# Strassen's scheme for half of the columns of a down projection, in a kernel for a two-layer trunk

## The chip, the cores and the metric

The kernel runs on one core of one Trainium2 chip. The metric is the device time in microseconds of one execution. The engines are TensorE (PE in the profile; PEld is its weight load), VectorE (DVE), ScalarE (ACT), GpSimd (POOL) and the sync engine's queue (SP), which issues the transfers of the weights. All data is float32. PE multiplies in the form fp32r, and each operand is split into a high part (hi, a copy in fp32r) and a low part (lo, the rest).

## The reference

Two layers over 256 tokens of width 2048. Each has a token mixer (a causal convolution in the first, a state-space layer with a gated output in the second) and then an MLP of width 8192:

```python
D_MODEL = 2048; SEQ = 256; DEPTH = 2; D_FF = 4 * D_MODEL

def mlp(h, w_up, w_down):
    a = jax.nn.relu(h @ w_up)
    return (a * a) @ w_down

def reference(x, ...):
    for i in range(DEPTH):
        h = rms_norm(x, mix_norm[i])
        x = x + (conv_module(h, ...) if i % 2 == 0 else ssm_module(h, ...))
        h = rms_norm(x, mlp_norm[i])
        x = x + mlp(h, mlp_w_up[i], mlp_w_down[i])
    return rms_norm(x, final_norm)
```

## The kernel before

`x` stays in SBUF as two blocks of 128 tokens by 2048 columns. Every dense projection is a list of steps (`self.steps`). One step is one piece of a weight of 1 MB: 8 row blocks of 128 by 256 columns for the up projection (`add_f`), 4 row blocks by 512 columns for the down projection (`add_t`). Each step has two halves of 128x1024 elements.

`run_steps` goes through the halves in order and keeps two kinds of work ahead of PE. `load` issues the transfers of the next four steps from the SP queue, into three raw buffers of a whole step. `split` makes hi on ACT (L118) and lo on DVE (L125; on POOL for the steps in `pool_lo`) for the next four halves; hi and lo have four buffers each. So the split of a half can begin when the matmuls of the half four places earlier have freed its buffer. The instructions of one engine run in the order in which a scheduler put them when the program was built; a tile framework adds the semaphores.

A down step multiplies in `mm_t` (L222 to L224): for each row block and each token block, three matmuls of 512 columns (activation hi by weight hi, hi by lo, lo by hi), 12 in a half. An up step (`mm_f`, L199 and L202) has 8 matmuls of 512 and 8 of 256 columns in a half.

The MLP takes the 8192 inner columns in eight row slices of 1024. `up(s)` makes slice s in four quarters of 256 columns; `relu2` (L807 to L812, and the hi and lo in L237 and L238) turns each quarter's result into squared activations `rT[s]`. `down(s)` multiplies them into four column slices of 512 columns, with one accumulator each in PSUM, which `add_x` adds to `x` on DVE (L820):

```python
        up(0)
        for s in range(1, nsl):
            up(s)
            down(s - 1)
        down(nsl - 1)
```

The second layer's MLP is the last large stage of the program.

Of the kernel before, what the change touches and what calls it, by code (L numbers as in the profile page):

```python
# [18 lines left out]
P = 128  # L19
EPS = 1e-6  # L20
D = 2048
T = 256
# [14 lines left out]
class Trunk:  # L37
    def __init__(self, ctx, tc, a, out):
# [10 lines left out]
        self.ms = pool("ms", 4, space=PSUM)  # L49
        self.dram = pool("dram", 1, space=DRAM)  # L50
        self.steps = []
        self.pending = []
        self.bg = []
        self.rate = self.credit = 0
        self.raws, self.parts = {}, {}
        self.loaded = 0
# [9 lines left out]
    def t4(self, shape, name="t4"):  # L66
        return self.tmp.tile(shape, F32, tag="t4", name=name)

# [11 lines left out]
    def add(self, view, shape, consume, pre=None):  # L80
        self.steps.append((view, shape, consume, pre))

    def add_f(self, w2d, k0, c0, consume, pre=None):
        self.add(w2d[k0 * P:(k0 + 8) * P, c0:c0 + 256].rearrange("(k p) n -> p k n", p=P), [P, 8, 256], consume, pre)
# [9 lines left out]
    def load(self, i, half=None):  # L94
        view, shape, _, _ = self.steps[i]
        for kind in self.before_load.pop(i, ()):
            self.table(*kind)
        if not half:
            self.raws[i] = self.w.tile(shape, F32, tag="raw", name="raw", bufs=3)
        raw = self.raws[i]  # L100
        nk = shape[1] // 2
        k = slice(0, shape[1]) if half is None else slice(half * nk, half * nk + nk)
        if len(shape) == 4:
            for j in range(shape[2]):
                self.fetch(raw[:, k, j, :], view[:, k, j, :])
        else:
            self.fetch(raw[:, k], view[:, k])
        self.loaded = i + 1

    def split(self, h, urgent=True):  # L110
        i, half = divmod(h, 2)
        raw = self.raws[i] if half == 0 else self.raws.pop(i)
        nk = raw.shape[1] // 2
        sl = raw[:, half * nk:(half + 1) * nk]
        hi = self.w.tile([P, nk] + list(raw.shape[2:]), F32R, tag="hi", name="hi", bufs=4)
        lo = self.w.tile([P, nk] + list(raw.shape[2:]), F32R, tag="lo", name="lo", bufs=4)
        with self.tc.high_priority(offset=URGENT if urgent else 0):
# [41 lines left out]
    def run_steps(self):  # L159
        n = 2 * len(self.steps)  # L160
        ns = 0
        for h in range(n):
# [7 lines left out]
            while self.loaded < min(len(self.steps), i + 4):  # L170
# [4 lines left out]
            if half == 0 and pre is not None:  # L175
                pre()
            hi, lo = self.parts.pop(h)
            consume(hi, lo, half)
            self.tick()
            self.pop_bg(self.rate)  # L180
# [504 lines left out]
    def mlp(self, layer, last_slice, last_block, hooks=None):  # L685
# [3 lines left out]

        def up(s):  # L690
            for q in range(4):
                for kc in range(2):
                    def consume(hi, lo, half, q=q, kc=kc):
                        if kc == 0 and half == 0:
                            if q == 0:
                                rT[s] = self.blk_tile([P, 8, 2, T], F32R, name="rT")
                            rT["acc"] = self.acc2()
                        A = rT["acc"]
                        self.mm_f([A[:, 0], A[:, 1]], self.hT, hi, lo, kc * 8 + half * 4,
                                  kc == 0 and half == 0, kc == 1 and half == 1)  # L700
                        if kc == 1 and half == 1:
                            if s == 0 and q == 1 and layer == 0:
                                self.rate = 2.75
                            if s == 0 and q == 0:
                                self.after(1, lambda: self.relu2(A, rT[s], 2 * q))
                            else:
                                self.relu2(A, rT[s], 2 * q)
                    self.add_f(w_up, kc * 8, s * 1024 + q * 256, consume)

        def down(s):  # L710
            for n in range(NS):
                by_block = s == nsl - 1 and n == NS - 1
                for kc in range(2):
                    def consume(hi, lo, half, n=n, kc=kc):
                        if kc == 0 and half == 0:
                            rT["acc"] = self.acc2()
                        k0 = kc * 4 + half * 2
                        self.mm_t(rT["acc"], lambda kk: rT[s][:, k0 + kk], hi, lo,
                                  kc == 0 and half == 0, kc == 1 and half == 1)
                        if kc == 1 and half == 1:  # L720
# [31 lines left out]
                    def consume_by_half(hi, lo, half, kc=kc):  # L752
# [3 lines left out]
                        for i, (b, c) in enumerate(((0, slice(0, 512)), (1, slice(0, 256)), (1, slice(256, 512)))):  # L756
                            with self.behind(self.mm_last):
                                self.mm_b(rT["acc"][i], lambda kk: rT[s][:, 2 * h + kk], hi, lo, b, c, h == 0, h == 3)
                            if h == 3:
# [6 lines left out]
                               (hooks or {}).get((nsl - 1 - s, n, kc)))  # L766

        up(0)
        for s in range(1, nsl):
            up(s)  # L770
            down(s - 1)
        down(nsl - 1)
# [43 lines left out]

    def tt(self, out, a, b, op):
# [788 lines left out]
```

## Time and profile before

| | |
|---|---|
| three runs | 1987.15, 1990.01, 1987.26 us; median 1987.26 |
| profiled execution, first to last instruction | span 1985.8 us (its time around the span isn't given apart) |
| mean granted clock of TensorE | 0.999 |
| PE, DVE, ACT, POOL busy | 99%, 71%, 48%, 14% of the span |
| second layer's MLP | about 1276 to 1976 us |
| transfers in the span | 428.49 MB, mean 216 GB/s |

An engine's busy time in the profile is the time in which one of its instructions ran. Matmuls overlap each other, so that their mean duration is longer than the distance from one start to the next. Rows of groups have the line, the engine, the operation and the tiles (out<-in), then the count, the busy time, the mean of one in ns, and the idle time just before them with what ended it. Rows of waits have who waited for whom, the time in all, how often, and the longest. Rows of the timeline have the start and the length in us. Rows of stretches have the busy time of PE, PEld, DVE, ACT and POOL, then the clock, the busy share of the transfer engines, and GB/s.

### The profile page before, as it was taken

What the parts mean: (1) busy time and instruction counts of PE and PEld (TensorE: products, weight loads), DVE (VectorE), ACT (ScalarE), POOL (GpSimd) and SP (SyncE); (2) the same over time, 40 slices, a digit from 0 to 9 for tenths busy, and PEclk for the clock granted to TensorE, in tenths of its full rate; (3) what the DMA queues carried; (4) which work ended last, traced back from release to release, by engine and by line L of the source; (5) the groups of instructions that cost most, each with busy time, mean ns of one, the idle gap of its engine ahead of it and who ended that gap; (6) DMA issues with size and microseconds to landing.
All of it is one profiled execution on the core that took longest, in us unless ns stands there. A gap on an engine that the chain in (4) does not pass through costs nothing.

```text
span 1985.8 us, 28885 instructions
## 1 busy us (share of the span) xinstructions
PE 1966.9 (99%) x11604; PEld 1687.0 (85%) x11604; DVE 1401.3 (71%) x1904; ACT 952.4 (48%) x1179; POOL 274.8 (14%) x252
## 2 busy tenths in 40 slices
PE   8999999999999999999999999999999999999998
PEld 8999788888888888888888788888888888888887
DVE  6899798888787777777558847565555565555655
ACT  6443655544444544444445445454444454444444
POOL 3998300000000221222010000000000000000000
PEclk9999999999999999999999999999999999999999
DMA  8767458667686877877898865665666656565653
GB/s 228 190 184 207 147 183 267 206 226 245 200 260 192 214 229 253 265 246 238 319 308 298 304 215 186 191 191 189 193 190 192 190 191 191 190 213 190 192 191 128
DMA packets 317030, 428.49 MB, mean 216 GB/s; under 512 B 9761, under 2 KB 211553, under 8 KB 313537
## 3 DMA queue, kind: packets, MB, share of 16 engines
q1 hardware_dynamic: 300976, 384.59, 61.6%
q0 software_dynamic: 12352, 37.49, 6.3%
q10 hardware_dynamic: 3568, 4.56, 0.8%
q8 instruction: 91, 1.49, 0.3%
q14 instruction: 43, 0.35, 0.1%
HBM read 400.08 MB, written 34.91 MB: 219 GB/s over the span
## 4 chain that ended last, share of the span: by engine, by line
PE 96%; DVE 2%; DMA 1%; issue 0%; SPq 0%; POOL 0%; ACT 0%; POOLq 0%; DVEq 0%; ACTq 0%
PE acc L199 24%; PE acc L222 15%; PE acc L223 15%; PE acc L224 15%; PE acc L202 12%; PE acc L213 3%; PE acc L212 3%; PE acc L211 3%; PE pk L484 1%; DMA Vt<-Vd 0%; SPq L92 0%; PE kp L1113 0%; PE xw L1254 0%; DMA raw<-in_conv_w_in_dram 0%; PE xt L254 0%
## 5 line engine op out<-in xcount | busy, mean ns | idle before, releaser
L118 ACT ACTIVATE hi<-raw 128x1024 fp32r<-128x1024 f32 x672 | 711.6, 1060 | 953.5 <-PE acc L224 510.2
L125 DVE TENSOR_TENSOR lo<-raw,hi 128x1024 fp32r<-128x1024 f32 x611 | 747.9, 1226 | 505.6 <-ACT hi L118 501.3
L199 PE MATMUL acc<-hT,hi 128*128 128x512 f32 x2048 | 514.4, 393 | 0.0
L199 PEld LDWEIGHTS acc<-hT,hi 128*128 128x128 f32 x2048 | 368.9, 189 | 68.0 <-issue 1.6
L222 PE MATMUL acc<-hi,rT 128*128 128x512 f32 x992 | 387.2, 391 | 0.0
L223 PE MATMUL acc<-lo,rT 128*128 128x512 f32 x992 | 386.4, 390 | 0.0
L224 PE MATMUL acc<-hi,rT 128*128 128x512 f32 x992 | 386.0, 389 | 0.0
L202 PEld LDWEIGHTS acc<-hT,lo 128*128 128x128 f32 x2048 | 279.6, 190 | 20.0
L202 PE MATMUL acc<-hT,lo 128*128 128x256 f32 x2048 | 286.3, 282 | 0.0
L222 PEld LDWEIGHTS acc<-hi,rT 128*128 128x128 f32 x992 | 186.3, 188 | 39.6 <-issue 1.6
L224 PEld LDWEIGHTS acc<-hi,rT 128*128 128x128 f32 x992 | 186.3, 188 | 39.1
L223 PEld LDWEIGHTS acc<-lo,rT 128*128 128x128 f32 x992 | 186.3, 188 | 38.0 <-issue 0.2
L125 POOL TENSOR_TENSOR lo<-raw,hi 128x1024 fp32r<-128x1024 f32 x60 | 143.1, 2402 | 31.3 <-ACT hi L118 24.8
L211 PE MATMUL acc<-hT,hi 128*128 128x256 f32 x512 | 146.1, 286 | 0.9 <-ACT hi L118 0.9
L212 PE MATMUL acc<-hT,hi 128*128 128x256 f32 x512 | 145.7, 286 | 0.3 <-DVE hT L259 0.3
L213 PE MATMUL acc<-hT,lo 128*128 128x256 f32 x512 | 145.5, 286 | 0.0
L829 DVE SCALAR_TENSOR_TENSOR cv<-vT,dw,cv 128x256 f32<-128x256 f32 x348 | 141.3, 486 | 2.2 <-ACT cv L527 1.7
L820 DVE TENSOR_TENSOR x<-x,acc 128x1024 f32<-128x1024 f32 (+1 forms) x72 | 83.6, 1161 | 27.6 <-PE acc L224 22.0
L211 PEld LDWEIGHTS acc<-hT,hi 128*128 128x128 f32 x512 | 98.9, 193 | 3.0 <-issue 1.6
L222 PE MATMUL acc<-hi,yT 128*128 128x512 f32 x256 | 101.1, 395 | 0.0
L212 PEld LDWEIGHTS acc<-hT,hi 128*128 128x128 f32 x512 | 98.8, 193 | 2.2 <-issue 1.6
L223 PE MATMUL acc<-lo,yT 128*128 128x512 f32 x256 | 99.9, 390 | 0.6 <-DVE lo L125 0.6
(285 smaller groups left out, 1722.9 us busy)
## 6 DMA issues: line engine op xcount, KB each, us to landing
raw<-in_mlp_w_up_dram SPq DMA_DIRECT2D x128, 1024.0 KB, 5.8
raw<-in_mlp_w_down_dram SPq DMA_DIRECT2D x128, 1024.0 KB, 5.2
raw<-in_ssm_w_glu_dram SPq DMA_DIRECT2D x32, 1024.0 KB, 5.5
raw<-in_conv_w_in_dram SPq DMA_DIRECT2D x60, 512.0 KB, 5.6
raw<-in_conv_w_out_dram SPq DMA_DIRECT2D x16, 1024.0 KB, 5.2
Vd<-bv POOLq DMA_DIRECT2D x16, 512.0 KB, 6.3
Md<-Kd POOLq DMA_DIRECT2D x32, 256.0 KB, 7.2
Wt<-Wd SPq DMA_DIRECT2D x8, 1024.0 KB, 10.1
```

The source lines that it names most:

```text
L118: self.nc.scalar.activation(hi, sl, AF.Copy)
L125: ins = eng.tensor_tensor(out=lo, in0=sl, in1=hi.bitcast(F32), op=ALU.subtract)
L199: mm(accs[m], lhsT=hi[:, kk, cs[m]], rhs=xT(k0 + kk), start=first and kk == 0, stop=False)
L202: mm(accs[m][:, 0:T], lhsT=lo[:, kk, cs[m]], rhs=xT(k0 + kk)[:, 0, :], start=False, stop=last and kk == 3)
L211: mm(accs[m], lhsT=hi[:, kk, c], rhs=x[:, 0, :], start=first and kk == 0, stop=False)
L212: mm(accs[m], lhsT=hi[:, kk, c], rhs=x[:, 1, :], start=False, stop=False)
L213: mm(accs[m], lhsT=lo[:, kk, c], rhs=x[:, 0, :], start=False, stop=last and kk == 3)
L222: mm(acc[:, b, :], lhsT=ak[:, 0, t], rhs=hi[:, kk, :], start=first and kk == 0, stop=False)
L223: mm(acc[:, b, :], lhsT=ak[:, 0, t], rhs=lo[:, kk, :], start=False, stop=False)
L224: self.mm_last = mm(acc[:, b, :], lhsT=ak[:, 1, t], rhs=hi[:, kk, :], start=False, stop=last and kk == 1)
L820: return self.nc.vector.tensor_tensor(out=out, in0=a, in1=b, op=op)
L829: return self.nc.vector.scalar_tensor_tensor(out=out, in0=a, scalar=s, in1=b, op0=op0, op1=op1)
```

## The change

In the second layer, for row slices 0 to 6, column slices 0 and 1 of the down projection are made together. The slice's activations A (256 tokens by 1024) are seen as 2 by 2 blocks: two token blocks by even and odd row blocks. The weight B (1024 by 1024 columns) is seen as 2 by 2 blocks: even and odd row blocks by two column slices. Seven products of block sums (Winograd's form of Strassen's scheme) take the place of eight products of blocks. Column slices 2 and 3 and row slice 7 stay as they were.

- `relu2_forms` takes the place of `relu2` for these slices. Beside the four blocks of A it makes S1 to S4 with four POOL sums of 128x128 and splits all eight: one more hi and lo of 128x512 for a quarter. One 512-wide operation takes the place of two 256-wide ones.
- The four blocks of B are loaded once, by four steps "x" that `add_block` notes. Steps "sum" make a block sum in place on POOL (L149), and then hi and lo as ever; step "held" uses a block again. Blocks B11 and B12 lie in a pool `wide` of four half buffers, which takes the memory of a pool that ends there; B21 and B22 lie in raw buffers until their last use.
- `products` has 6 matmuls for a half. Four PSUM banks p, r, q, t hold the products; each is added to blocks of `x` on DVE with `take` or `both` (six adds of 128x512, one of 128x1024).
- The products are spread over the next slice's up projection: first quarter, product 1, second quarter, products 2 and 3, third quarter, 4 and 5, column slice 2, fourth quarter, 6 and 7, column slice 3.
- In this layer, the lo of the up projection's second and fourth quarters is made on POOL.
- For the whole kernel, raw buffers are six of half a step instead of three of a whole, and each half has a transfer of its own.

```diff
@@ load: buffers of half a step
-            self.raws[i] = self.w.tile(shape, F32, tag="raw", name="raw", bufs=3)
...
+        for hf in (0, 1) if half is None else (half,):
+            k = slice(hf * nk, hf * nk + nk)
+            size = [P, nk] + list(shape[2:])
+            if key is not None and key[-1] in self.in_wide:
+                raw = self.wide.tile(size, F32, tag="wd", name="raw")
+            else:
+                raw = self.w.tile(size, F32, tag="raw", name="raw", bufs=6)
...
@@ split
+        elif pre == "sum":
+            key, a, b, op = key
+            sl = self.blocks[key + (half,)]
+            self.nc.gpsimd.tensor_tensor(out=sl, in0=self.blocks[a + (half,)], in1=self.blocks[b + (half,)], op=op)
...
@@ mlp
+        def products(acc, s, i, hi, lo, half, first):
+            mm = partial(self.nc.tensor.matmul, acc, skip_group_check=True)
+            for jj in range(2):
+                F = rT[s][half][:, jj]
+                mm(lhsT=F[:, 0, i, :], rhs=hi[:, jj, :], start=first and half == jj == 0, stop=False)
+                mm(lhsT=F[:, 0, i, :], rhs=lo[:, jj, :], start=False, stop=False)
+                self.mm_last = mm(lhsT=F[:, 1, i, :], rhs=hi[:, jj, :], start=False, stop=half == jj == 1)
...
+            return [lambda: load(B(0, 0), key(0), part(A11, "p", True, take(c11, "p"))),
+                    lambda: (load(B(0, 1), key(1)),
+                             total(key(0), key(1), key(0), ALU.subtract, part(S1, "r", True, take(c22, "r")))),
+                    lambda: load(B(1, 0), key(2), part(A12, "q", True, take(c11, "q"))),
+                    lambda: (load(B(1, 1), key(3)),
+                             total(key(0), key(3), key(0), ALU.subtract, part(S2, "p", False, take(c12, "p")))),
+                    lambda: load_done(key(3), part(S4, "r", False, take(c12, "r"))),
+                    lambda: total(key(2), key(0), key(2), ALU.subtract, part(A22, "t", True, take(c21, "t", ALU.subtract))),
+                    lambda: total(key(1), key(3), key(1), ALU.subtract, part(S3, "p", False, both))]
...
+                    if layer and q % 2:
+                        self.pool_lo.add(len(self.steps))
...
+        formed = lambda s: layer == 1 and s < nsl - 1
...
+            m = seven(s - 1, 0)
+            for q, part in enumerate((m[0:1], m[1:3], m[3:5], m[5:7])):
+                up(s, 2 * q)
+                up(s, 2 * q + 1)
+                for e in part:
+                    e()
+                if q > 1:
+                    down(s - 1, q)
...
+    def relu2_forms(self, acc, R):
...
+        nc.scalar.activation(t, acc[:, :, T:2 * T], AF.Copy)
+        nc.vector.tensor_tensor(out=t, in0=acc[:, :, 0:T], in1=t, op=ALU.add)
+        nc.vector.scalar_tensor_tensor(out=t, in0=t, scalar=0.0, in1=self.rstdB.broadcast_to([P, 2, T]),
+                                       op0=ALU.max, op1=ALU.mult)
...
+        pt(out=v[:, 0, :], in0=a21, in1=a22, op=ALU.add)
+        pt(out=v[:, 1, :], in0=v[:, 0, :], in1=a11, op=ALU.subtract)
+        pt(out=v[:, 2, :], in0=a11, in1=a21, op=ALU.subtract)
+        pt(out=v[:, 3, :], in0=a12, in1=v[:, 1, :], op=ALU.subtract)
+        self.hsplit(u, R[:, 0, 0:4, :], R[:, 1, 0:4, :])
+        self.hsplit(v, R[:, 0, 4:8, :], R[:, 1, 4:8, :])
```

Two places show how the order on the engines changes. The first is POOL in the MLP. Before, nothing of the MLP stands on it; these are its last rows, from the state-space layer (`xr`, `S`, `m`) over the norm ahead of the MLP (L286) to the end.

```order
L1165 COPY xr<-xJ 128x8x8x16
L1229 MEMSET S 128x32
L1207 TENSOR_TENSOR rb_9813<-ssa,mhalf 128x2
L1282 MEMSET m 128x16 x4
L286 TENSOR_TENSOR rstd<-ssm,mhalf 128x2
L1521 DMA gF<-in_final_norm_dram 128x2048
L797 TENSOR_TENSOR rb<-ssb,mhalf 128x1
```

Now, in the middle of the MLP, around products 4 and 5 of a slice. `raw_13328` and `raw_13330` are the two halves of B11 (by now B12 - B11), `raw_13470` and `raw_13472` of B12, `raw_13496` and `raw_13498` of B21, `raw_13606` and `raw_13608` of B22. DMAHW are semaphores of transfers.

```order
L960 TENSOR_TENSOR v_13580<-u_13579 128x128 [waits Activation_49]
L962 TENSOR_TENSOR v_13580<-u_13579 128x128
L961 TENSOR_TENSOR v_13580<-v_13580,u_13579 128x128 [waits Pool_49]
L963 TENSOR_TENSOR v_13580<-u_13579,v_13580 128x128 [waits Pool_49]
L149 TENSOR_TENSOR raw_13328<-raw_13606,raw_13328 128x1024 [waits DMAHW7_49]
L149 TENSOR_TENSOR raw_13470<-raw_13606,raw_13470 128x1024
L149 TENSOR_TENSOR raw_13330<-raw_13608,raw_13330 128x1024 [waits DMAHW0_49]
L149 TENSOR_TENSOR raw_13472<-raw_13608,raw_13472 128x1024
L149 TENSOR_TENSOR raw_13496<-raw_13328,raw_13496 128x1024 [waits DMAHW1_49,Pool_49]
L149 TENSOR_TENSOR raw_13498<-raw_13330,raw_13498 128x1024 [waits DMAHW2_49,DVE_49,Pool_49]
```

The sums for products 4, 7 and 6 stand in one row as soon as B22 has landed: product 4's first half, 7's first, 4's second, 7's second, then both halves for 6.

The second place is DVE. Before, an up projection's quarter in the middle of a slice: L125 makes lo, L808, L810 and L238 are `relu2`.

```order
L125 TENSOR_TENSOR lo<-raw,hi 128x1024 x3
L808 TENSOR_TENSOR t<-acc,t 128x512
L810 SCALAR_TENSOR_TENSOR t<-t,bcs 128x256 x2
L125 TENSOR_TENSOR lo<-raw,hi 128x1024
L238 TENSOR_TENSOR rT<-u,rT 128x2x256
```

Now, from product 2 to the column slice behind product 5: L162 makes lo, L954, L281 and L953 are `relu2_forms`, L968 adds a product to `x`.

```order
L954 SCALAR_TENSOR_TENSOR t<-t,bcs 128x512
L162 TENSOR_TENSOR lo<-raw,hi 128x1024
L968 TENSOR_TENSOR x<-x,mr 128x512
L162 TENSOR_TENSOR lo<-raw,hi 128x1024 x2
L968 TENSOR_TENSOR x<-x,mq 128x512
L281 TENSOR_TENSOR rT<-u,rT 128x512
L162 TENSOR_TENSOR lo<-raw,hi 128x1024
L281 TENSOR_TENSOR rT<-v,rT 128x512
L162 TENSOR_TENSOR lo<-raw,hi 128x1024 x4
L953 TENSOR_TENSOR t<-acc,t 128x512
L162 TENSOR_TENSOR lo<-raw,hi 128x1024
L968 TENSOR_TENSOR x<-x,mp 128x512
```

The adds of products 2 and 3 (`mr`, `mq`) stand between the lo of the third quarter's halves; the four lo in one row are those of products 4 and 5, and behind them comes the third quarter's `relu2_forms`. The transfers of B22's two halves wait on the SP queue for raw buffers that the first two lo of the third quarter free.

More of the change, by code (lines that the diff above doesn't have):

```diff
@@ L1 @@
 from contextlib import ExitStack, nullcontext
+from functools import partial
 import math
@@ L50, in __init__ @@
         self.dram = pool("dram", 1, space=DRAM)
+        self.ctx = ctx
+        self.t4_guard = tc.tile_pool(name="quad", bufs=4)
+        self.quad = self.t4_guard.__enter__()
+        self.wide = None
         self.steps = []
@@ L94, in load @@
     def load(self, i, half=None):
-        view, shape, _, _ = self.steps[i]
+        view, shape, _, pre = self.steps[i]
         for kind in self.before_load.pop(i, ()):
             self.table(*kind)
-        if not half:
-            self.raws[i] = self.w.tile(shape, F32, tag="raw", name="raw", bufs=3)
-        raw = self.raws[i]
-        nk = shape[1] // 2
[L102 to L107, printed above, removed]
@@ L161, in run_steps @@
         ns = 0
+        count = [0]
+        for step in self.steps:
+            count.append(count[-1] + (step[3] not in ("sum", "held")))
+        self.ahead = lambda i: count[i]
         for h in range(n):
@@ L169, in run_steps @@
                 pre, ns = None, self.presplit
-            while self.loaded < min(len(self.steps), i + 4):
+            while self.loaded < len(self.steps) and self.ahead(self.loaded) < self.ahead(i) + 4:
                 self.load(self.loaded)
@@ L174, in run_steps @@
                 ns += 1
-            if half == 0 and pre is not None:
+            if half == 0 and callable(pre):
                 pre()
+            if consume is None:
+                continue
             hi, lo = self.parts.pop(h)
```

120 lines of the change are left out of this document (101 added, 19 removed).

## The prediction

> **What bounds the kernel now.** I read the busy table and the chain of the page first, then the stretch of the second layer's MLP (1276 to 1976 us), then its waits, then single rows.
>
> ```profile
> PE 1966.9 (99%) x11604; PEld 1687.0 (85%) x11604; DVE 1401.3 (71%) x1904; ACT 952.4 (48%) x1179; POOL 274.8 (14%) x252
> PE 96%; DVE 2%; DMA 1%; issue 0%; SPq 0%; POOL 0%; ACT 0%; POOLq 0%; DVEq 0%; ACTq 0%
> ...
> 0.00:20.00 20.00, 14.19 (x88) 13.43 (x88) 13.64 (x36) 13.39 (x27) 0.80 (x7) 1.00 0.95 275
> 1050.00:1200.00 150.00, 146.07 (x1355) 120.06 (x1354) 106.60 (x128) 72.24 (x97) 1.01 (x5) 1.00 0.75 268
> 1276.00:1976.00 700.00, 700.00 (x3573) 598.76 (x3572) 414.64 (x426) 325.62 (x367) 1.46 (x3) 1.00 0.60 188
> ...
> DVE lo L125 <- ACT hi L118: 264.9, 214, 2.5
> ACT hi L118 <- PE acc L224: 197.4, 122, 2.1
> ACT hi L118 <- PE acc L199: 166.3, 123, 2.4
> SPq L92 <- DVE lo L125: 613.7, 121, 6.3
> ```
>
> PE is the chain. In the MLP stretch it is busy for all of the 700 us at clock 1.00, while DVE has 285 us free, ACT 374, and POOL does nothing. The waits run backwards from PE: ACT waits for a matmul to free a hi buffer, DVE waits for ACT, the DMA queue waits for DVE to free a raw buffer. So PE's instruction count sets this stretch, and the other engines have room, on average.
>
> **What one matmul is worth.** The mean duration of a matmul (0.39 us) overlaps its neighbours, so I use the distance between starts.
>
> ```profile
> 1460.36 0.39 PE L222 MATMUL acc<-hi,rT 128*128 128x512 f32 x1
> ...
> 1463.08 0.39 PE L222 MATMUL acc<-hi,rT 128*128 128x512 f32 x1
> ...
> 1294.36 1.84 PE acc L199 x8
> 1296.20 0.95 PE acc L202 x8
> 1297.15 1.84 PE acc L199 x8
> ```
>
> From 1460.36 to 1463.08 lie 12 down matmuls (one half step): 2.72 us, 0.2267 each. A half step of the up projection takes 1.84 + 0.95 = 2.79 us.
>
> **Removed and added on PE.** Per row slice, two column slices cost 2 x 48 = 96 matmuls of 512 columns; seven products cost 7 x 12 = 84. Seven slices do so: 84 matmuls fewer, with the same shapes and one weight load each. 84 x 0.2267 = 19.04 us, or 2.72 us per slice of 16 x 2.79 + 16 x 2.72 = 88.2 us. The Trainium skill (TensorE: Matmul & The Clock Gate, Back-to-back issue gap) gives 512/2.4 + 2.5 = 216 ns for an isolated warm matmul, by which the saving would be 18.1 us; the rows above say 227.
>
> **Added on the other engines, per slice.**
>
> ```profile
> L125 DVE TENSOR_TENSOR lo<-raw,hi 128x1024 fp32r<-128x1024 f32 x251 | 307.5, 1225 | 265.5 <-ACT hi L118 264.9 <-PE acc L202 0.6
> L118 ACT ACTIVATE hi<-raw 128x1024 fp32r<-128x1024 f32 x251 | 266.2, 1061 | 366.5 <-PE acc L224 197.4 <-PE acc L199 166.3 <-issue 2.2
> L820 DVE TENSOR_TENSOR x<-x,acc 128x1024 f32<-128x1024 f32 x31 | 37.9, 1221 | 12.3 <-PE acc L224 12.3
> L810 DVE SCALAR_TENSOR_TENSOR t<-t,bcs 128x256 f32<-128x256 f32 x64 | 24.4, 422 | 1.0
> L238 DVE TENSOR_TENSOR rT<-u,rT 128x512 fp32r<-128x512 f32 x32 | 22.2, 692 | 0.2 <-ACT rT L237 0.2
> L808 DVE TENSOR_TENSOR t<-acc,t 128x512 f32<-128x512 f32 x32 | 21.9, 684 | 0.0
> L237 ACT ACTIVATE rT<-u 128x512 fp32r<-128x512 f32 x32 | 20.3, 633 | 1.0
> L812 ACT ACTIVATE u<-t 128x512 f32<-128x512 f32 x32 | 19.8, 620 | 0.4 <-DVE t L810 0.4
> L807 ACT ACTIVATE t<-acc 128x512 f32<-128x512 f32 x32 | 18.8, 586 | 0.0
> ...
> L125 POOL TENSOR_TENSOR lo<-raw,hi 128x1024 fp32r<-128x1024 f32 x60 | 143.1, 2402 | 31.3 <-ACT hi L118 24.8 <-DVE rowsel L896 6.4
> L400 POOL TENSOR_TENSOR x<-x,bo 128x1024 f32<-128x1024 f32 x4 | 9.6, 2391 | 0.0
> L286 POOL TENSOR_TENSOR rstd<-ssm,mhalf 128x2 f32<-128x2 f32 x3 | 2.1, 705 | 245.5 <-DVE ssm L284 245.5
> ```
>
> - ACT: 38 weight halves instead of 32 (14 for the products, 8 before): 38 x 1.06 = 40.3. Four relu2 groups with one more 512-wide copy: 4 x (0.586 + 0.620 + 2 x 0.633) = 9.9. Sum 50 of about 85.5 us.
> - DVE: 30 lo (8 of the up halves go to POOL): 36.8. Relu2: 4 x (0.684 + 2 x 0.422 + 2 x 0.692) = 11.6. Adds to x: two of 1.22, six 512-wide at 0.68 (the 512-wide row from PSUM), one of 1.22 = 7.7. Sum 56 (53 before).
> - POOL: 8 lo and 8 sums of weight blocks at 2.40 = 38.4, and 16 sums of 128 x 128. No row has that form. Its low end is an eighth of 2.40, 0.30; its high end the two-column operation at 0.705. Sum 43 to 50. I take 0.4, nearer the first because both are plain adds: 45.
> - DMA moves the same bytes, in 512 KB pieces instead of 1 MB, for all weights of the kernel.
>
> None of them is full on average. What decides is whether a half is ready when PE comes, since a product's half lasts only 6 x 0.2267 = 1.36 us, while ACT needs 1.06 and DVE 1.23 for one.
>
> **The walk through one slice.** Splits run four halves ahead of PE (four hi and lo buffers). I put t = 0 at the start of the second product; 0.2 us from the last matmul's start to the release of its buffer, 0.1 per hand-over. PE without stalls: second and third product to 5.44, third quarter of the up projection to 16.6, fourth product to 19.3, fifth to 22.05, then a plain column slice. Around the second and third product DVE owes four lo, two adds and a relu2: 4.9 + 1.4 + 2.9 = 9.2 us in 5.44; the next halves last 2.79 each, so this backlog of 4 us is worked off with no deadline missed (lo of the next halves done at 3.9, 5.8, 7.1, 9.7; PE needs them at 5.4, 8.2, 11.0, 13.8). The same holds after the sixth and seventh.
>
> The tight place is the fourth product. Its sum needs block B22, whose two loads wait for raw buffers freed by those lo at 3.9 and 5.8. The length of a 512 KB load:
>
> ```profile
> raw<-in_mlp_w_down_dram SPq DMA_DIRECT2D x64, 1024.0 KB, 5.1
> raw<-in_mlp_w_up_dram SPq DMA_DIRECT2D x59, 1024.0 KB, 5.8
> q1 hardware_dynamic: 95832, 129.66, 59.2%
> ```
>
> No single 512 KB row stands in this stretch. Half of the shorter, 2.6 us, is the low end; the longer, 5.8, the high end. The engines move 188 GB/s at a busy share of 0.60, so 313 GB/s when busy: 512 KB is 1.7 us of transfer, and 5.1 less 3.35 leaves 1.75 fixed. That is 3.4; with the queue's issue and hand-overs I take 4.1. B22 is there at 8.1 and 10.0. On POOL the built order puts six sums in a row: fourth product half 0 (to 10.5), seventh half 0 (12.9), fourth half 1 (15.3), then three more. The fourth product's second half has its hi at 16.5 and its lo at 17.7; PE asks for the hi at 18.0 and for the lo at 18.2. ACT and DVE are in order, so the fifth product follows: lo at 18.9 and 20.2, needed at 19.6 and 21.1; then the plain slice's first lo at 22.1 against 22.3. Everything is in time, by 0.2 to 0.7 us. For what such a walk leaves out I allow 0.2 us per slice, 1.4 in all. With 5.8 us for the load, the fourth product waits 0.9 and the plain slice 0.5 more: 1.4 per slice, 9.8 in all. With 2.6 there is no wait.
>
> At the first product's sum of the next block row, and at the sixth and seventh, there is no such place: their sums are done 12 us or more ahead, and the POOL lo of the up halves take 2.40 against 2.79 of PE.
>
> **Elsewhere.** The 512 KB loads start earlier than the 1 MB ones could, since one half's buffer is enough. PE lacks 5.8 us in the first 20 and 3.9 between 1050 and 1200, both places with DMA waits; I take zero, with a gain of up to 3 or a loss of up to 2 by reordering.
>
> **Sum.** 1985.8 - 19.0 + 1.4 = 1968.2 of span. The median, 1987.26, lies 1.5 above the span (the page gives the profiled execution's span alone): 1969.7, rounded to 1969.5.
>
> **Rivals.**
> 1. The fourth product's chain is late by a buffer's turn, as worked out for a load of 5.8 us: 1969.5 - 1.4 + 9.8 = 1978. For it: the spare of 0.2 to 0.7. Against: the central load time has 1.7 us less.
> 2. Slower: the same chain waits over 2.72 us per slice, and the saving is gone. That needs B22 about 3.4 us later than I take it, or POOL sums at 3.5 instead of 2.40 (three stand in the chain). At 4.5 us a slice: 1987.3 + 7 x 1.8 = 2000. The likeliest way to it is that DVE and POOL take turns on operations that read two operands from SBUF. DVE's lo, relu2 and copies of that kind are 36.8 + 4 x (0.844 + 1.384) = 45.7 us; with POOL's 45 that is 90.7 against 85.5 us of PE, so at least 88.2 + 2.5 per slice, and 2005. Against it:
>
> ```profile
> 154.20 26.04 POOL L125 TENSOR_TENSOR lo<-raw,hi 128x1024 fp32r<-128x1024 f32 x11
> ...
> 151.87 9.50 DVE L829 SCALAR_TENSOR_TENSOR cv<-vT,dw,cv 128x256 f32<-128x256 f32 x24
> ```
>
> While POOL ran eleven lo in 26.04 us (2.37 each), DVE ran 24 two-operand instructions in 9.50 us, 0.40 each, without one pause of 2.4. The Trainium skill (SBUF — State Buffer, Who interferes with whom) states that a DVE instruction with two SBUF inputs and a GpSimd instruction that reads SBUF contend for a shared port, and that one of them blocks wholly. By that rule this rival would be the forecast; these two rows disagree with it.
> 3. The loads gain elsewhere too, and nothing waits: 1969.5 - 1.4 - 3 = 1965.
>
> **Chances.** As forecast (1966 to 1973) 0.58; rival 1 and shades of it (1973 to 1983) 0.24; rival 3 (under 1966) 0.07; saving just eaten 0.05; rival 2 0.06. About 0.2% (4 us) is what a measurement here can tell from no change. Faster 0.89, same 0.05, slower 0.06. The range 1964.5 to 1980 holds the first, most of rival 1 and most of rival 3: 0.8.
>
> **What would show it.** PE with 11520 matmuls; product matmuls 0.227 us apart; a slice of about 85.6 us; POOL near 45 us busy per slice; DVE's lo still 1.22. A wrong walk shows as idle PE before the fourth or fifth product or the slice behind them, put down to ACT hi or DVE lo, with POOL's sum or a load behind it. If DVE and POOL take turns, lo on DVE grows past 1.3 us or POOL's sums past 2.5. If PE is idle elsewhere, the forecast is wrong by a wait that I did not see.

## The result and the profile after

The changed kernel takes 2040.09 us (median of 4 runs, 2039.47 to 2040.84) against 1987.2 for the kernel before: a ratio of 1.026, 95% interval 1.025 to 1.028. It is slower by 53 us, and 71 above the forecast of 1969.5. The page's busy table and chain:

```profile
PE 1981.1 (97%) x11520; PEld 1680.7 (82%) x11520; DVE 1553.7 (76%) x1917; ACT 1002.5 (49%) x1249; POOL 708.6 (35%) x484
...
PE 81%; DVE 5%; POOL 5%; issue 4%; DMA 2%; ACT 1%; SPq 0%; DVEq 0%; POOLq 0%; ACTq 0%
```

PE has its 11520 matmuls, as planned, and is idle for 56.7 us of 2037.8 instead of 18.9. The chain now runs through DVE, POOL and DMA as well, 12% of it in all. Until the second MLP little changed: the norm's `rstd` ahead of it starts at 1275.4 us instead of 1276.1. The starts of the first product in two successive row slices, in the timeline (start, duration), tell what a slice costs:

```profile
1424.59 0.40 PE L737 MATMUL mp<-hi,rT 128*128 128x512 f32 x1
...
1521.08 0.40 PE L737 MATMUL mp<-hi,rT 128*128 128x512 f32 x1
```

96.5 us, where 85.6 was forecast and 88.2 stood before. The table by stretches tells what the engines do in 180 us, nearly two slices (busy time and count of PE, PEld, DVE, ACT, POOL, then the granted clock):

```profile
1510.00:1690.00 180.00, 167.51 (x823) 138.92 (x822) 144.04 (x102) 89.19 (x102) 115.32 (x61) 0.96 0.52 167
```

DVE is busy for 144 of 180 us, POOL for 115, yet PE is idle for 12.5, and its granted clock is 0.96. Groups of instructions in the second MLP (1276 to 2028 us):

```profile
L162 DVE TENSOR_TENSOR lo<-raw,hi 128x1024 fp32r<-128x1024 f32 x230 | 384.9, 1693 | 86.2 <-ACT hi L155 86.0
...
L162 POOL TENSOR_TENSOR lo<-raw,hi 128x1024 fp32r<-128x1024 f32 x63 | 166.2, 2661 | 12.2 <-ACT hi L155 11.8 <-ACT hT L301 0.4
L149 POOL TENSOR_TENSOR raw<-raw 128x1024 f32<-128x1024 f32 x56 | 161.6, 2911 | 101.9 <-DMA raw<-in_mlp_w_down_dram 97.2 <-DVE lo L162 4.6
...
L281 DVE TENSOR_TENSOR rT<-v,rT 128x512 fp32r<-128x512 f32 x28 | 43.9, 1567 | 30.0 <-ACT rT L280 30.0
...
L968 DVE TENSOR_TENSOR x<-x,acc 128x1024 f32<-128x1024 f32 x17 | 20.8, 1221 | 25.6 <-PE acc L833 24.5 <-PE acc L267 1.1
```

DVE's lo, 1.225 before, has a mean of 1.69; the split of `v` takes 1.57 instead of 0.69; POOL's sums take 2.91 instead of 2.39. All of these read two operands from SBUF. The add of a PSUM bank to `x` (L968) still takes 1.22. The waits of the same stretch (in total, times, longest):

```profile
ACT hi L155 <- POOL raw L149: 53.3, 14, 5.1
...
PEld mp L738 <- DVE lo L162: 26.1, 13, 4.9
...
PE mp L738 <- DVE lo L162: 20.0, 10, 4.6
...
PE mr L738 <- DVE lo L162: 6.9, 8, 1.8
```

What reaches PE is mostly the wait for the lo of product 4 (`mp`, 20.0 us), then for that of product 5 (`mr`, 6.9). The timeline there, with POOL's six sums in one row and what DVE does meanwhile:

```profile
1545.73 17.90 POOL L149 TENSOR_TENSOR raw<-raw 128x1024 f32<-128x1024 f32 x6
...
1545.89 2.78 DVE L281 TENSOR_TENSOR rT<-u,rT 128x512 fp32r<-128x512 f32 x1
...
1548.60 3.42 DVE L162 TENSOR_TENSOR lo<-raw,hi 128x1024 fp32r<-128x1024 f32 x1
...
1551.94 2.86 DVE L281 TENSOR_TENSOR rT<-v,rT 128x512 fp32r<-128x512 f32 x1
...
1554.73 11.12 DVE L162 TENSOR_TENSOR lo<-raw,hi 128x1024 fp32r<-128x1024 f32 x4
...
1558.14 0.79 PE L738 MATMUL mp<-lo,rT 128*128 128x512 f32 x1 [4.62 <-DVE lo L162]
...
1558.74 0.63 PE L739 MATMUL mp<-hi,rT 128*128 128x512 f32 x1
...
1559.16 0.63 PE L737 MATMUL mp<-hi,rT 128*128 128x512 f32 x1
...
1565.10 0.39 PE L739 MATMUL mr<-hi,rT 128*128 128x512 f32 x1
...
1565.33 0.39 PE L737 MATMUL mr<-hi,rT 128*128 128x512 f32 x1
```

Beside the 17.9 us of the six sums (2.98 each) DVE gets through little more than one operation to a sum: a split in 2.78, a lo in 3.42, a split in 2.86, four lo in 11.12, the last of which runs behind the sums and takes 1.21. Undisturbed these seven take 7.5 us. PE waits 4.62 for the first lo of product 4, and more behind it. After the wait its matmuls stand 0.42 apart, later 0.23 again.

So the loss, against the best run below with the same 11520 matmuls (PE idle for 19.1 and busy for 1947.9 us of a span of 1967.0), is 37.6 us of idle PE and 33.2 of matmuls that last longer: 70.8 in all.

### The profile page after: what moved, and what is told of

It reads as the page before. It is cut to its first block, busy times and chain, and to the rows that moved or that the text cites. A ratio compares the mean times of both kernels' runs of the same rounds, so it can differ in the third digit from the quotient of the medians.

```text
span 2037.8 us, 30146 instructions
## 1 busy us (share of the span) xinstructions
PE 1981.1 (97%) x11520; PEld 1680.7 (82%) x11520; DVE 1553.7 (76%) x1917; ACT 1002.5 (49%) x1249; POOL 708.6 (35%) x484
## 4 chain that ended last, share of the span: by engine, by line
PE 81%; DVE 5%; POOL 5%; issue 4%; DMA 2%; ACT 1%; SPq 0%; DVEq 0%; POOLq 0%; ACTq 0%
PE acc L242 18%; PE acc L265 10%; PE acc L266 10%; PE acc L267 10%; PE acc L245 9%; PE acc L833 7%; DVE lo L162 3%; PE acc L254 3%; PE acc L256 3%; PE acc L255 3%; POOL lo L162 2%; DMA raw<-in_mlp_w_down_dram 2%; POOL raw L149 1%; ACT hi L155 1%; PE pk L527 1%
## 5 line engine op out<-in xcount | busy, mean ns | idle before, releaser
L155 ACT ACTIVATE hi<-raw 128x1024 fp32r<-128x1024 f32 x714 | 752.3, 1058 | 889.8 <-PE acc L267 333.7
L162 DVE TENSOR_TENSOR lo<-raw,hi 128x1024 fp32r<-128x1024 f32 x589 | 823.4, 1406 | 324.2 <-ACT hi L155 322.6
L242 PEld LDWEIGHTS acc<-hT,hi 128*128 128x128 f32 x2048 | 370.3, 189 | 69.3 <-issue 1.6
L162 POOL TENSOR_TENSOR lo<-raw,hi 128x1024 fp32r<-128x1024 f32 x124 | 313.1, 2543 | 252.7 <-ACT hi L155 246.0
L265 PE MATMUL acc<-hi,rT 128*128 128x512 f32 x544 | 212.9, 392 | 0.0
L266 PE MATMUL acc<-lo,rT 128*128 128x512 f32 x544 | 212.1, 390 | 0.0
L267 PE MATMUL acc<-hi,rT 128*128 128x512 f32 x544 | 211.7, 389 | 0.0
L149 POOL TENSOR_TENSOR raw<-raw 128x1024 f32<-128x1024 f32 x56 | 161.6, 2911 | 101.9 <-DMA raw<-in_mlp_w_down_dram 97.2
L833 PE MATMUL acc<-hi,rT 128*128 128x512 f32 x448 | 141.5, 392 | 0.0
L265 PEld LDWEIGHTS acc<-hi,rT 128*128 128x128 f32 x544 | 102.1, 188 | 22.6 <-issue 1.6
L267 PEld LDWEIGHTS acc<-hi,rT 128*128 128x128 f32 x544 | 102.1, 188 | 21.4
L266 PEld LDWEIGHTS acc<-lo,rT 128*128 128x128 f32 x544 | 102.1, 188 | 21.0 <-issue 0.2
L254 PEld LDWEIGHTS acc<-hT,hi 128*128 128x128 f32 x512 | 98.8, 193 | 3.4 <-issue 2.1
```

The source lines that it names most:

```text
L149: self.nc.gpsimd.tensor_tensor(out=sl, in0=self.blocks[a + (half,)], in1=self.blocks[b + (half,)], op=op)
L155: self.nc.scalar.activation(hi, sl, AF.Copy)
L162: ins = eng.tensor_tensor(out=lo, in0=sl, in1=hi.bitcast(F32), op=ALU.subtract)
L242: mm(accs[m], lhsT=hi[:, kk, cs[m]], rhs=xT(k0 + kk), start=first and kk == 0, stop=False)
L254: mm(accs[m], lhsT=hi[:, kk, c], rhs=x[:, 0, :], start=first and kk == 0, stop=False)
L265: mm(acc[:, b, :], lhsT=ak[:, 0, t], rhs=hi[:, kk, :], start=first and kk == 0, stop=False)
```

## The experiments

Three theories stood at the start. Theory 1: a DVE operation with two SBUF inputs and a POOL operation take turns, and that is the loss. Theory 2: the chain from B22's load over POOL's sums to product 4 is late by itself, as in the prediction's rival 1. Theory 3: only the order of the sums is at fault. In this section "the changed kernel" is the one above, and ratios are to the kernel before.

**1. Without the sums.**

```diff
-            self.nc.gpsimd.tensor_tensor(out=sl, in0=self.blocks[a + (half,)], in1=self.blocks[b + (half,)], op=op)
```

> Left out: the block sums of the down projection's weights on POOL (each product uses one of the blocks as it is); all else is the changed kernel. Theory 1 (DVE's operations with two SBUF inputs and POOL's take turns, and both together want more than a slice's time): the shared work falls from 91 to about 71 us per slice, so the slice goes from 96 back to 86 us, DVE's lo from 1.69 to about 1.3, the time to 1968-1978. Theory 2 (the in-order chain load of B22, three sums, product 4 is late by itself) and theory 3 (only the order of the sums is bad) expect the same 1968-1978, since the chain goes with the sums. If the time stays above 2010, the sums are not the cause and all three fall.

1968.86 us, ratio 0.991 (0.989 to 0.992), slices 85.5 us apart. The stretch shown above of the changed kernel has PE busy throughout:

```profile
1510.00:1690.00 180.00, 180.00 (x917) 153.89 (x917) 121.56 (x119) 102.60 (x118) 73.59 (x53) 1.00 0.60 191
```

So without the sums PE keeps the pace that the prediction gave, with the 512 KB loads and POOL's other work in place (lo still has a mean of 1.32 beside that work); the sums are the cause, in one way or another.

**2. POOL fills instead of adding.** Each sum becomes an add of 8 columns, which keeps the wait for the loads, and two fills.

```diff
-            self.nc.gpsimd.tensor_tensor(out=sl, in0=self.blocks[a + (half,)], in1=self.blocks[b + (half,)], op=op)
+            p, q = self.blocks[a + (half,)], self.blocks[b + (half,)]
+            self.nc.gpsimd.tensor_tensor(out=sl[:, 0, 0:8], in0=p[:, 0, 0:8], in1=q[:, 0, 0:8], op=op)
+            for _ in range(2):
+                self.nc.gpsimd.memset(sl, 0.01)
```

> Left out: of each block sum only the first 8 columns of the half are summed; then POOL fills the half twice with a constant. POOL is as busy (about 2.4 us for a half), has to wait for the same loads and stands in the same order, but reads almost nothing of SBUF. Theory 1 (turns): DVE's lo goes from 1.69 back to 1.25-1.35, the stall at products 4 and 5 shrinks from 10 us a slice to under 2, time 1968-1985. Theories 2 (load and in-order chain) and 3 (order of the sums): the chain is unchanged, the slice stays at 93-96 us, time 2020-2042.

2004.31 us, ratio 1.009 (1.007 to 1.010): between what theory 1 and what theories 2 and 3 expected, and in neither range. DVE's lo is back at a mean of 1.37, but the edit had moved POOL's order as well, as the timeline shows:

```profile
1540.74 5.41 POOL L152 MEMSET raw<- 128x1024 f32 x6
...
1544.40 2.95 ACT L158 ACTIVATE hi<-raw 128x1024 fp32r<-128x1024 f32 x3 [4.92 <-POOL raw L152]
```

Fills of several halves stand mixed in the first row, 0.90 us each; ACT has waited 4.92 us when it gets product 4's second half at 1544.40, behind four of them. This run mixes two causes, and experiments 5 and 6 part them.

**3. The sums for products 6 and 7 later.**

```diff
+            with self.behind(self.lo_ins) if key[2] in (1, 2) else nullcontext():
```

> Nothing left out. The four sums for products 6 and 7 are issued on POOL only behind the newest lo, so two sums instead of six stand ahead of product 4's second half. Theory 3 (only the order is bad): the stall goes, slice 86 us, time 1968-1978. Theory 2: one sum of 2.4 us leaves the chain; about 0.2 to 0.7 us of slack comes back, 1968-1985. Theory 1 (turns): the order helps at products 4 and 5, but the shared work is still 91 to 96 us in a slice of 85.5, so it comes back at another place: slice 91-95 us, 2005-2035.

2040.60 us. The edit did nothing: `behind` orders instructions of one engine, and the newest lo is on DVE. POOL still runs its six sums in one row, so this is the changed kernel again and tells nothing of theory 3.

**4. All on DVE, the sums for products 6 and 7 behind the newest lo.** POOL has no tensor work in this MLP.

```diff
-            self.nc.gpsimd.tensor_tensor(out=sl, in0=self.blocks[a + (half,)], in1=self.blocks[b + (half,)], op=op)
+            with self.behind(self.lo_ins) if key[2] in (1, 2) else nullcontext():
+                self.nc.vector.tensor_tensor(out=sl, in0=self.blocks[a + (half,)], in1=self.blocks[b + (half,)], op=op)
...
-                    if layer and q % 2:
-                        self.pool_lo.add(len(self.steps))
...
-        pt = nc.gpsimd.tensor_tensor
+        pt = nc.vector.tensor_tensor
```

> Nothing left out. POOL does no tensor work in the second MLP: the block sums, the lo of the up projection's second and fourth quarters and the sums of activations stand on DVE, the sums for products 6 and 7 late as in the run before. DVE's work by its undisturbed rows: 38 lo x 1.225 + 8 sums x 1.22 + 16 small sums x 0.2 + relu2 11.3 + adds 7.7 = 78.5 us of 85.5. Theory 1 (turns): more work on DVE, but nothing to wait for: lo back at 1.23, slice 86-87.5 us, time 1968-1982, faster than both kernels. Against it: if DVE's slowness came from its own load (port traffic of DMA and ACT, not POOL), lo stays near 1.7 and DVE, at over 95 us a slice, sets the time: above 2040.

2034.10 us, ratio 1.023 (1.022 to 1.025). Every lo takes 1.22 again, so what slowed it was POOL, not DVE's own load. But the expected time is missed: products 4 and 5 no longer wait, and products 6 (`mt`) and 7 do. The timeline there:

```profile
1481.77 1.23 DVE L163 TENSOR_TENSOR lo<-raw,hi 128x1024 fp32r<-128x1024 f32 x1 [1.20 <-ACT hi L156]
...
1482.91 1.22 DVE L150 TENSOR_TENSOR raw<-raw 128x1024 f32<-128x1024 f32 x1
...
1483.05 0.50 PE L739 MATMUL mt<-lo,rT 128*128 128x512 f32 x1 [0.76 <-DVE lo L163]
...
1485.85 1.22 DVE L163 TENSOR_TENSOR lo<-raw,hi 128x1024 fp32r<-128x1024 f32 x1
```

A sum (L150) stands between two lo, and PE, which uses up a half in 1.36 us, waits for the lo. So a burst on one engine alone can stall PE too.

**5 and 6. The sums in the order of need, adding or filling.** A pair that differs in nothing but what POOL reads. In both:

```diff
+            with self.behind(self.sum_ins) if self.sum_ins is not None else nullcontext():
+                self.sum_ins = self.nc.gpsimd.tensor_tensor(out=sl, in0=self.blocks[a + (half,)], in1=self.blocks[b + (half,)], op=op)
```

and in the second the 8 columns and two fills of experiment 2, each behind the one before.

> Nothing left out. The sums now stand on POOL in the order in which the products need them: both halves of product 4's, then 6's, then 7's (before, 7's first half stood ahead of 4's second). Theory 3 (only the order of the sums is at fault): product 4's second half is ready one sum earlier, the stall at products 4 and 5 goes from 10 us a slice to under 3, time 1968-1990. Theory 1 (DVE and POOL take turns): POOL's six sums still run beside the seven DVE operations that PE waits for, one DVE operation to a sum; slice 92-96 us, time 2015-2040.

> Left out: of each block sum only the first 8 columns of the half are summed; POOL then fills the half twice with a constant (0.95 us each), and the sums stand in the order of the run before. So POOL is as long busy with a sum (2.1 to 2.5 us), waits for the same loads and stands in the same order as there; only its reading of SBUF is gone. Theory 1 (turns): DVE's lo at 1.25-1.35, time 1968-1985, and the distance to the run before is what the turns cost. Theory 2 (the load of B22 is late by itself, 12 us after the start of product 2 instead of 10): the stall stays at 1 to 3 us a slice, 1976-1992. Above 2000 the chain on POOL would be the cause whatever it reads.

Groups of the second MLP in the run that adds:

```profile
L164 DVE TENSOR_TENSOR lo<-raw,hi 128x1024 fp32r<-128x1024 f32 x230 | 384.9, 1690 | 94.8 <-ACT hi L157 94.6
...
L151 POOL TENSOR_TENSOR raw<-raw 128x1024 f32<-128x1024 f32 x56 | 165.7, 2982 | 99.4 <-DMA raw<-in_mlp_w_down_dram 94.5 <-DVE lo L164 4.6
```

The same of the run that fills:

```profile
L168 DVE TENSOR_TENSOR lo<-raw,hi 128x1024 fp32r<-128x1024 f32 x230 | 309.1, 1358 | 109.7 <-ACT hi L161 109.4
...
L155 POOL MEMSET raw<- 128x1024 f32 x112 | 107.0, 955 | 6.4
```

And its timeline at products 4 and 5:

```profile
1527.81 1.97 POOL L155 MEMSET raw<- 128x1024 f32 x2
1528.71 3.50 DVE L168 TENSOR_TENSOR lo<-raw,hi 128x1024 fp32r<-128x1024 f32 x3 [1.34 <-ACT hi L161]
```

Adding: 2044.65 us, ratio 1.029 (1.027 to 1.030), just above the range that theory 1 gave. Filling: 1970.65, ratio 0.991 (0.990 to 0.993). In the second run POOL is busy nearly as long with a sum (two fills of 0.955 and an add of 0.32 are 2.23, against 2.39 for an undisturbed sum), waits for the same loads and has the same order. While it fills, three lo follow each other in 3.50 us; while it adds, a lo waits. 74.0 us lie between the two: that is what the turns with the block sums cost, with the lower clock behind the stalls (see below) in it. POOL's lo and small sums still take turns with DVE in both runs, which is why the mean of lo is 1.358 and not 1.22 in the second. Theory 3 falls with 2044.65, since the better order gives nothing back while the turns are there. Of theory 2 little is left: 1970.65 is 1.8 us above experiment 1, and the runs of the two overlap (1969.72 to 1971.03, 1967.42 to 1969.81). What the chain costs in the old order without turns is not shown; experiment 2, 35.4 us above experiment 1, has mixed fills in it.

The Trainium skill (SBUF — State Buffer, Who interferes with whom) says that a DVE instruction with two SBUF inputs contends with a GpSimd instruction that reads SBUF, not with one that only writes it. The two runs agree on both halves: a mean lo of 1.690 beside the sums, and three lo of 3.50 together beside the fills.

**7. All on DVE, the sums spread.** The four sums for products 6 and 7 leave `split` and are issued by `run_steps` one at a time, two in column slice 2 and two in the fourth quarter.

```diff
+        if key[2] in (1, 2):
+            for half in (0, 1):
+                self.early[i - 3, half] = partial(self.block_sum, key, a, b, op, half)
...
+            if (i, half) in self.early:
+                with self.behind(self.lo_ins):
+                    self.early[i, half]()
```

> Nothing left out. No tensor work on POOL in the second MLP, as in the run with all on DVE, but the four sums for products 6 and 7 are taken out of the place just ahead of product 6, where that run lost its time, and stand one by one between the lo made during column slice 2 and the fourth quarter. DVE's work is 78.5 us of a slice of 85.5. Theory 1: with POOL silent, every DVE operation takes its undisturbed time, and only a burst of more work than the four buffers cover can stall PE; with the burst spread, slice 85.5-87 us, time 1968-1980, faster than both kernels. If DVE at 92% of a slice can't be scheduled so tightly, the gaps of 1.2 us at products 6 and 7 stay: 2000-2035.

1975.35 us, ratio 0.994 (0.992 to 0.995): 12 us below the kernel before, as expected, and 59 us under experiment 4 by the place of four instructions in a slice.

**8. POOL copies instead of adding.** As experiment 2, with `tensor_copy(sl, q)` in place of each fill.

> Left out: of each block sum only the first 8 columns of the half are summed; POOL then copies one block over the half, twice: an operation with one SBUF input in place of two. It measures what POOL's reading of one operand does to DVE. If any POOL operation that reads SBUF shuts out DVE's operations with two SBUF inputs: lo mean 1.6-1.8 us, as in the changed kernel, single lo up to 3.4, and a time of 2020-2060. If only POOL's operations with two inputs do: lo 1.25-1.4 and 1970-1990.

2128.48 us, one run, above both expected times. The time says nothing of the turns: POOL's order moved here too, and sums wait for one another in new places. The mean of lo up to 2028 us, 1.42, lies between the two expectations and doesn't decide either. The single rows do. The timeline at products 4 and 5, and the lo in it with the next one (shortest, median and longest time):

```profile
1474.75 6.34 DVE L168 TENSOR_TENSOR lo<-raw,hi 128x1024 fp32r<-128x1024 f32 x4
...
1476.85 2.03 POOL L155 COPY raw<-raw 128x1024 f32<-128x1024 f32 x1
...
L168 DVE TENSOR_TENSOR lo<-raw,hi x5: 1219/1828/2051, 1474.8 to 1481.6; 128x1024 fp32r<-128x1024 f32 x5
```

The fills' line, with copies in it (shortest, median and longest time of one):

```profile
L155 POOL COPY raw<-raw x108: 1032/1045/2057, 1322.7 to 2016.9; 128x1024 f32<-128x1024 f32 x108
```

A copy takes 1.045 (the median) and up to 2.06 beside DVE. Of the four lo of the timeline, 1.58 each from the first to the last, the two beside a copy of a whole block take 1.83 and 2.05 instead of 1.22; each ends 1.08 us behind the copy. So an operation with one SBUF input takes turns too; its turn is shorter.

**9 and 10. The same total of shared work, in two places.** Experiment 9 is experiment 5 with all lo on DVE; experiment 10 is experiment 7 with the lo of the second and fourth quarters and the small sums on POOL.

```diff
  experiment 9
-                    if layer and q % 2:
-                        self.pool_lo.add(len(self.steps))
  experiment 10
+                    if layer and q % 2:
+                        self.pool_lo.add(len(self.steps))
-        pt = nc.vector.tensor_tensor
+        pt = nc.gpsimd.tensor_tensor
```

> Nothing left out. The changed kernel with its sums on POOL in the order of need, but the lo of the up projection's second and fourth quarters back on DVE. That takes 8 POOL operations of 2.4 us out of a slice and adds 8 DVE operations of 1.22. Work that takes turns, by undisturbed rows: DVE 38 x 1.225 + 4 x 2.23 = 55.5, POOL 8 x 2.40 + 4 x 1.6 = 25.6, together 81 of a slice of 85.5 us. If the total is what counts, PE is no longer stalled: 1970-1985. If the place counts (six sums of 2.4 us in a row beside the seven DVE operations that PE waits for next), the stall at products 4 and 5 stays as it is: slice 94-97 us, 2025-2045.

> Nothing left out. The mirror of the run before: the sums stand on DVE, spread as in the run with DVE spread, and POOL keeps the lo of the up projection's second and fourth quarters and the small sums of activations. Work that takes turns: DVE 30 x 1.225 + 8.9 + 8 x 1.22 = 55.5, POOL 8 x 2.40 + 6.4 = 25.6, again 81 us in a slice. The place differs: POOL's lo come at PE's pace of 2.79 us in the quarters of the up projection, where DVE is ahead. If the place counts: no stall, lo on DVE 1.3, 1968-1980. If the total counts, the same time as the run before, whatever that is.

The timeline of experiment 9 at products 4 and 5:

```profile
1542.89 12.77 DVE L164 TENSOR_TENSOR lo<-raw,hi 128x1024 fp32r<-128x1024 f32 x4 [0.58 <-ACT hi L157]
1544.55 13.35 POOL L151 TENSOR_TENSOR raw<-raw 128x1024 f32<-128x1024 f32 x4
```

The same stretch of 180 us, first of experiment 9, then of experiment 10:

```profile
1510.00:1690.00 180.00, 166.74 (x831) 139.63 (x830) 150.48 (x122) 91.93 (x105) 79.66 (x48) 0.99 0.53 171
...
1510.00:1690.00 180.00, 178.13 (x906) 150.62 (x905) 138.08 (x129) 97.69 (x111) 75.20 (x51) 1.00 0.60 191
```

Experiment 9: 2027.57 us, ratio 1.020 (1.018 to 1.022). Experiment 10: 1979.65, ratio 0.996 (0.995 to 0.998). By undisturbed rows both have 81 us of shared work in a slice, and they lie 48 us apart. In experiment 9 POOL makes four sums in 13.35 us, and DVE the four lo that PE needs next in 12.77. The total did not decide, the place did: in experiment 10 POOL is busy for 75 us of the stretch, DVE's lo take 1.31 in the mean, and PE still loses only 1.9 us, which fits POOL's operations falling where DVE is ahead.

**11. All four sums in column slice 2.**

```diff
-                self.early[i - 3, half] = partial(self.block_sum, key, a, b, op, half)
+                self.early[i - 4, half] = partial(self.block_sum, key, a, b, op, half)
```

> Nothing left out. The run with all on DVE and the sums spread, with all four sums for products 6 and 7 between the lo made during column slice 2 (two of them before in the fourth quarter). There PE lost 1 to 1.7 us a slice in column slice 2, the fourth quarter and product 6. If DVE is late at product 6 because of the two sums in the quarter: 1970-1974. If column slice 2 is already full (4 lo, an add, relu2 and now four sums: 13.5 us of work in 10.9): 1976-1985.

The page's busy table:

```profile
PE 1947.9 (99%) x11520; PEld 1670.4 (85%) x11520; DVE 1551.8 (79%) x2149; ACT 1005.3 (51%) x1249; POOL 276.4 (14%) x252
```

DVE's lo in the second MLP (shortest, median and longest time of one):

```profile
L172 DVE TENSOR_TENSOR lo<-raw,hi x293: 1215/1222/1229, 1275.2 to 1949.1; 128x1024 fp32r<-128x1024 f32 x147
```

The stretch shown above of the changed kernel:

```profile
1510.00:1690.00 180.00, 179.45 (x913) 152.87 (x912) 154.42 (x185) 101.92 (x116) 0.00 (x0) 1.00 0.59 189
```

1969.70 us, ratio 0.991 (0.990 to 0.992): the forecast time, with all of the computation. DVE is busy for 154 of 180 us, more than in the changed kernel, PE for 179.45 at clock 1.00, and POOL not at all. Of its 293 lo the slowest takes 1.229.

**12. The small sums on POOL again.** Experiment 7 with `pt = nc.gpsimd.tensor_tensor`.

> Nothing left out. The run with all on DVE and the sums spread, but the 16 small sums of activations on POOL again (0.46 us each there by undisturbed rows, about 0.2 on DVE). DVE has 3.2 us less in a slice, POOL 7 us. If small POOL operations cost DVE only short turns: 1970-1975, a little faster. If each takes a turn of DVE's that is as long as itself: 7 us of turns for 3.2 saved, 1975-1985.

1978.61 us, ratio 0.996 (0.995 to 0.997): 3.3 above experiment 7, though DVE has less to do. The 112 small sums take 0.284 us each on DVE in experiment 7, 31.7 in all; without them DVE's busy time falls only by 9.4 us (1550.4 to 1541.0), so turns take back most of the saving. DVE is less busy for all that, and ACT now waits 61.4 us for POOL's last small sum (`v`). Which of the two makes the kernel longer is not shown. The spread of the two runs nearly touches (1973.15 to 1977.14 and 1978.05 to 1983.55), so the sign is better known than the size.

## Why the prediction was wrong

- **PE's saving** was right: 11520 matmuls, 85.5 us a slice where none waits (85.6 forecast), and experiments 11, without turns, and 6, without those of the block sums, end at 1969.70 and 1970.65.
- **The place** was right: "the tight place is the fourth product".
- **The step that failed** is the rejection of rival 2. It named the turns, and worked out 90.7 us of shared work in a slice, and then put them aside by two rows of the conv stage, eleven lo on POOL beside 24 quick `cv<-vT,dw,cv` on DVE. But `cv` is a PSUM bank (`acc = self.bank([P, T], name="cv")`, L525 of the kernel before), so of its two blocks only `vT` lies in SBUF, and the rows don't bear on the question. The Trainium skill's rule (SBUF — State Buffer, Who interferes with whom), which the prediction weighed against them, agrees with experiments 5 and 6; the disagreement was a misreading.
- **The rows that do bear on it** were there. Of 611 lo on DVE in the trace before, two ran beside a POOL operation on a whole block, a copy of 1.04 us:

```profile
1027.54 1.04 POOL L1165 COPY xr<-xJ 128x1024 f32<-128x1024 f32 x1 [4.07 <-DMA xJ<-xs]
...
1027.82 1.84 DVE L125 TENSOR_TENSOR lo<-raw,hi 128x1024 fp32r<-128x1024 f32 x1
...
1045.05 1.04 POOL L1165 COPY xr<-xJ 128x1024 f32<-128x1024 f32 x1 [8.41 <-DMA xJ<-xs]
1045.23 1.94 DVE L125 TENSOR_TENSOR lo<-raw,hi 128x1024 fp32r<-128x1024 f32 x1 [1.60 <-ACT hi L118]
```

  They took 1.84 and 1.94 instead of 1.22. The first ends 1.08 us after the copy does, as if it had begun only about then. (A third ran beside the last 0.2 us of a two-column operation and took 1.225.) The prediction quoted the mean of 1.225 of the second MLP's 251 lo, among which these two don't stand.
- **The terms that follow from it.** POOL's sum, taken as 2.40, measured 2.91; DVE's lo, taken as 1.225, measured 1.69; a small sum on POOL, taken as 0.4, had a mean of 0.7 to 1.1. The walk's allowance of 0.2 us a slice became 96.5 - 85.6 = 10.9.
- **Rival 2's own time** (2005) was too low as well: it reckoned with the total and left out the clock. The turns came in one burst of six sums at the place with the least spare; experiments 9 and 10 show what the place is worth.
- **A term that was missing**: PE's clock. Two stretches of 6 us, the first of the changed kernel behind its wait of 4.62 us, the second of experiment 4, and the row with the longest of experiment 4's waits of PE in this MLP:

```profile
1557.00:1563.00 6.00, 4.86 (x11) 3.40 (x12) 6.00 (x3) 1.77 (x3) 6.00 (x3) 0.50 0.00 0
...
1489.00:1495.00 6.00, 5.51 (x12) 4.15 (x13) 6.00 (x9) 4.71 (x6) 0.00 (x0) 0.50 0.61 178
...
PE mp L739 <- DVE lo L163: 9.1, 7, 1.7
```

  The granted clock is 0.50, and the matmuls stand 0.42 to 0.43 apart instead of 0.23. In the changed kernel's second MLP the trace has the clock at half for 57.8 us, in one or two stretches of each slice. So at most 28.9 of the 33.2 us by which the matmuls last longer come from the clock; the rest was not parted further. The Trainium skill (TensorE: Matmul & The Clock Gate, What's actually happening) says that the array falls to half its clock after about one idle window of 3.4 us. The wait of 4.62 us agrees. But in experiment 4 no wait is over 1.7 us, and the clock is halved all the same: several short waits close together are enough.
- **Rival 1** (late by a buffer's turn) and rival 3 (loads gain elsewhere): in experiment 6, in the slice of its timeline, the loads of B22 land 9.3 and 11.9 us after the start of product 2, by the landing times of the trace, where the walk had 8.1 and 10.0. So B22 is late by about what rival 1 supposed, and with the sums in the order of need this cost at most the 1.8 us above experiment 1. Elsewhere the gain is under 1 us, the 0.7 by which the second MLP begins earlier.
- **Two small terms of the walk** were off without moving the result. It had 0.3 us from the last matmul's start over the freed buffer to ACT's next hi (0.2 and 0.1), figures that no row gives; in the trace before it is 0.43 (a matmul of L224 at 1462.85, hi at 1463.28). And a load later by 1.7 us makes product 4 wait 1.2 by the walk's own times (17.7 + 1.7 - 18.2), not 0.9.

## What to carry to other kernels

Work moved from DVE to POOL was no relief here, where both read SBUF and DVE's operations have two SBUF inputs: it cost 2.4 us of shared time for 1.22 of DVE's, and of the kernels that leave nothing out the fastest had POOL silent and DVE at 86%. Before you judge by a pair of rows whether two engines disturb each other, look up in which memory each operand lies, and compare the slowest instances of one operation, not its mean. Where PE takes halves at nearly the pace at which they are made, place a burst where the buffers are ahead: four instructions in another place of a slice moved this kernel by 59 us.

## What was not expected of the hardware

- With operations of this kind waiting on both engines they take turns, one DVE operation to one POOL operation. A turn of both lasts a little less than the two alone: a lo and a sum (1.22 + 2.39 = 3.61) took 3.42, a split and a sum (0.69 + 2.39 = 3.08) 2.78 to 2.86.
- The page of the profile counts an instruction that waits for its turn as busy. DVE's 1553.7 and POOL's 708.6 us of the changed kernel hold this waiting: in experiment 11, DVE does all of POOL's work of this MLP too and is busy for 1551.8.
- Fills on POOL left DVE's lo at 1.22 (experiment 6); copies on POOL, with one input, drew it out to as much as 2.05 (experiment 8).
- PE's clock was halved behind waits of 1.7 us and less that came close together (experiment 4).
